# A weight-gradient matmul: one slice instead of two over the hardware queues, three more warm-up matmuls, and another order of the parts from slice 12 on

## The chip, the cores and the metric

The kernel runs on one core of a Trainium2 chip. The time is the device time of one execution in microseconds. Ten executions of the kernel before took 176.77 to 177.47 us; their median is 176.97 us.

## The reference

The input has the shape 16 x 512 x 1024 and the output's gradient 16 x 512 x 768, both float32. The result is the gradient of the weights, 1024 x 768, float32:

```python
grad_weight = np.einsum('bmk,bmn->kn', input, grad_output)
```

Batch and rows together make 8192 rows, which are summed over. So this is one product, the transposed input (1024 x 8192) times the gradient (8192 x 768).

## The kernel before, in words

The 8192 rows are cut into S = 64 slices of 128 rows. A slice has an X part (128 x 1024, from the input) and a G part (128 x 768, from the gradient). TensorE multiplies in bfloat16 and sums in float32 in PSUM, which has eight banks of 128 x 512 float32. Each slice takes twelve matmuls of 128 x 128 by 128 x 512. They belong to three parts of four groups each, and each group needs a bank of its own:

- part A, the output rows 0 to 511 and the columns 0 to 511: the weights of the matmul are four 128-column pieces of X, the moving side is G's first 512 columns (`wide_mm`, L129 to L132);
- part B, the same for the output rows 512 to 1023;
- part N, the output columns 512 to 767, turned: the weights are two 128-column pieces of G, the moving side is each half of X (`narrow_mm`, L134 to L143).

Three parts need twelve banks, and there are eight. So a part is opened, takes in some slices, and is closed: its four sums are evacuated from PSUM, and its banks go to the end of the list `free`. The first evacuation of a part is a copy, shared between VectorE and ScalarE (`copy_out`, L123); each later one is an addition on VectorE into `acc` or `acct` in SBUF (`add_out`, L120).

The order of the work is written out by hand. The scheduler is set to keep the program's order on TensorE, VectorE and ScalarE (L67). `ORDER` (L16) is a list of steps: "B15" means that part B takes in slices up to number 15 (not included), "AB16" that A and B take turns slice by slice, and "!" that the parts are closed after the last slice. After slice 12 the parts are opened and closed in turn up to slices 19, 31 and 50, and N takes the slices 31 to 63 in one run at the end of `ORDER`. A loop then finishes A and B (L210 to L222): for each of the eight groups it runs the slices 50 to 63 into one bank, adds the bank to `acc` and stores the result through the SyncE queue. The last group is cut into pieces of 256, 128 and 128 columns. N's result is turned by VectorE (L183) and stored through ScalarE's queue (L204).

The slices reach SBUF in two ways. Slices 0 and 1 come as float32 over the two hardware queues: SyncE issues G (L73, L75, L77), ScalarE issues X (L74, L76, L78). Each is then rounded to bfloat16 by VectorE and ScalarE in pieces of 256 columns (`round_pair`, L102; `round_slice`, L106). Slice 1's last 256 G columns (`gn1`, L89) and all of the slices 2 to 63 come over GpSimd's software queue, which rounds on the way in (L94 for G, L95 for X). The tiles `gt` and `xt` have 42 buffers each. At most eight transfers of this queue are in flight: each waits for the landing of the one eight places before it.

Before its first data has landed, TensorE runs nine 128 x 512 matmuls on constants into a bank that nobody reads (L84, L85).

Of the kernel before, what the change touches and what calls it, by code (L numbers as in the profile page):

```python
# [8 lines left out]
P = 128  # L9
NA = 512  # L10
SQ = 32

ORDER = (  # L16
    "A1! N1 B2! N2 A2 N3! A3 B3 A4! B5 N5 B6! N7 A6 N8! A9! B10 N9 B12! N12! A12! "
    "B15 A15 AB16 A19! B19! N19! A22 B22 AB28 A31! B31! N31! A34 B34 AB47 A50! B50! N64!"
).split()

HW = 2
WARMUP = 9
XBUFS = 42


# [1 line left out]
def kernel(  # L27
# [6 lines left out]
    nc = tc.nc  # L34
    bf16 = mybir.dt.bfloat16
    f32 = mybir.dt.float32

    B, M, K = input.shape
    _, _, N = grad_output.shape
    S = B * M // P  # L40
    KS = K // P
    NB = N - NA
# [3 lines left out]
    X = input.rearrange("b m k -> (b m) k")  # L46
    G = grad_output.rearrange("b m n -> (b m) n")
    OUT = out.rearrange("(ks p) n -> p ks n", p=P)

    head = ctx.enter_context(tc.tile_pool(name="head", bufs=1))  # L50
    xg = ctx.enter_context(tc.tile_pool(name="xg", bufs=XBUFS))
    accp = ctx.enter_context(tc.tile_pool(name="accp", bufs=1))
    psum = ctx.enter_context(tc.tile_pool(name="psum", bufs=1, space=bass.MemoryType.PSUM))
# [5 lines left out]
    turned = accp.tile([P, K // SQ, SQ, NT], f32, name="turned")  # L59


    xs = [None] * S
    gwide = [None] * S
    gnarrow = [None] * S
# [1 line left out]
    E = mybir.EngineType  # L66
    ctx.enter_context(tc.manual_schedule(engines={E.PE, E.DVE, E.Activation}))  # L67

    xf = [head.tile([P, K], f32, name=f"xf{s}") for s in range(HW)]
    gf = [head.tile([P, NA], f32, name=f"gf{s}") for s in range(HW)]  # L70
    gnf = head.tile([P, NB], f32, name="gnf")
    rows = [slice(s * P, (s + 1) * P) for s in range(HW)]
    nc.sync.dma_start(out=gf[0], in_=G[rows[0], 0:NA])  # L73
    nc.scalar.dma_start(out=xf[0][:, 0:NA], in_=X[rows[0], 0:NA])  # L74
    nc.sync.dma_start(out=gnf, in_=G[rows[0], NA:N])  # L75
    nc.scalar.dma_start(out=xf[0][:, NA:K], in_=X[rows[0], NA:K])  # L76
    nc.sync.dma_start(out=gf[1], in_=G[rows[1], 0:NA])  # L77
    nc.scalar.dma_start(out=xf[1], in_=X[rows[1], :])  # L78


    ones = nc.const_aps.tensor(1.0, (P, P), bf16)
    ones_wide = nc.const_aps.tensor(1.0, (P, NA), bf16)
    wps = psum.tile([P, NA], f32, name="bank7")
    for i in range(WARMUP):  # L84
        nc.tensor.matmul(wps, ones, ones_wide, start=(i == 0), stop=(i == WARMUP - 1))  # L85


    gn1 = head.tile([P, NB], bf16, name="gn1")
    nc.gpsimd.dma_start(out=gn1, in_=G[rows[1], NA:N])  # L89
    gnarrow[1] = gn1  # L90
    for s in range(HW, S):
        gt = xg.tile([P, N], bf16, name="gt")
        xt = xg.tile([P, K], bf16, name="xt")
        nc.gpsimd.dma_start(out=gt, in_=G[s * P : (s + 1) * P, :])  # L94
        nc.gpsimd.dma_start(out=xt, in_=X[s * P : (s + 1) * P, :])  # L95
        xs[s] = xt
        gwide[s] = gt[:, 0:NA]
        gnarrow[s] = gt[:, NA:N]

    QX = 256  # L100

    def round_pair(dst, src, c):  # L102
        nc.vector.tensor_copy(out=dst[:, c : c + QX], in_=src[:, c : c + QX])  # L103
        nc.scalar.copy(out=dst[:, c + QX : c + 2 * QX], in_=src[:, c + QX : c + 2 * QX])  # L104

    def round_slice(s):  # L106
        gt = head.tile([P, NA], bf16, name=f"g{s}")
        xt = head.tile([P, K], bf16, name=f"x{s}")
        round_pair(gt, gf[s], 0)

        for c in (0, NA) if s == 0 else (NA, 0):
            round_pair(xt, xf[s], c)
            if s == 0 and c == 0:
                gn0 = head.tile([P, NB], bf16, name="gn0")
                nc.vector.tensor_copy(out=gn0, in_=gnf)
                gnarrow[0] = gn0
        xs[s] = xt
        gwide[s] = gt

    def add_out(dst, src):  # L120
        nc.vector.tensor_add(out=dst, in0=src, in1=dst)  # L121

    def copy_out(dst, src, i):  # L123
        if i % 2 == 0:
            nc.vector.tensor_copy(out=dst, in_=src)  # L125
        else:
            nc.scalar.copy(out=dst, in_=src)  # L127

    def wide_mm(bank, k, s, start, stop, c0=0, c1=NA):  # L129
        nc.tensor.matmul(  # L130
            bank, xs[s][:, k * P : (k + 1) * P], gwide[s][:, c0:c1], start=start, stop=stop
        )  # L132
# [12 lines left out]
    class Part:  # L145
        def __init__(self, matmul, groups, dst):
            self.matmul = matmul
            self.groups = groups
            self.dst = dst
            self.done = 0  # L150
            self.first = True
            self.banks = None

    wide_dst = lambda k: acc[:, k, :]
    narrow_dst = lambda t, h: acct[:, t, h * NA : (h + 1) * NA]
    parts = {
        "A": Part(wide_mm, [(k,) for k in range(KS // 2)], wide_dst),
        "B": Part(wide_mm, [(k,) for k in range(KS // 2, KS)], wide_dst),
        "N": Part(narrow_mm, [(t, h) for h in range(KH) for t in range(NT)], narrow_dst),
    }  # L160
    free = [f"bank{i}" for i in range(8)]

    def one_slice(part, close):
        s = part.done
        part.done += 1
        if s < HW and xs[s] is None:
            round_slice(s)
        opened = part.banks is None
        if opened:
            names = [free.pop(0) for _ in part.groups]  # L170
            part.banks = [(name, psum.tile([P, NA], f32, name=name)) for name in names]
        for i, (group, (name, bank)) in enumerate(zip(part.groups, part.banks)):
            part.matmul(bank, *group, s, opened, close)
            if close:
                dst = part.dst(*group)
                if part.first:
                    copy_out(dst, bank, i)
                else:
                    add_out(dst, bank)
                if part is parts["N"] and s == S - 1:  # L180
                    t, h = group
                    hb = NA // SQ
                    nc.vector.transpose(  # L183
                        out=turned[:, h * hb : (h + 1) * hb, :, t],
                        in_=dst.rearrange("p (b r) -> p b r", r=SQ),
                    )
                free.append(name)
        if close:
            part.banks = None
            part.first = False  # L190

    for step in ORDER:
        close = step.endswith("!")
        names = step.rstrip("!").rstrip("0123456789")
        upto = int(step.strip("ABN!"))
        while any(parts[n].done < upto for n in names):
            for n in names:
                if parts[n].done < upto:
                    one_slice(parts[n], close and parts[n].done == upto - 1)

    rows_of = out.rearrange("(b r) n -> r b n", r=SQ)
    for a in range(P // SQ):
        c = NA + a * NT * SQ
        nc.scalar.dma_start(  # L204
            out=rows_of[:, :, c : c + NT * SQ],
            in_=turned[a * SQ : (a + 1) * SQ].rearrange("p b r t -> p b (r t)"),
# [3 lines left out]
    for k in range(KS):  # L210
        slices = range(parts["A" if k < KS // 2 else "B"].done, S)
        pieces = [(0, NA)] if k < KS - 1 else [(0, 256), (256, 384), (384, NA)]
        for c0, c1 in pieces:
            name = free.pop(0)
            bank = psum.tile([P, NA], f32, name=name)[:, 0 : c1 - c0]
            for s in slices:
                wide_mm(bank, k, s, s == slices[0], s == slices[-1], c0, c1)
            add_out(acc[:, k, c0:c1], bank)
            free.append(name)
            W = NB if k < 4 else c1 - c0  # L220
            for c in range(c0, c1, W):
                nc.sync.dma_start(out=OUT[:, k, c : c + W], in_=acc[:, k, c : c + W])  # L222

# [29 lines left out]
```

## Time and profile before

| | us |
|---|---|
| median of ten runs | 176.97 |
| lowest, highest | 176.77, 177.47 |
| the profiled execution, its own time | 176.86 |
| its span, first to last instruction | 175.1 |
| TensorE busy (matmuls) | 170.4 |
| VectorE busy | 53.9 |
| ScalarE busy | 6.7 |
| GpSimd busy (issuing transfers) | 66.6 |

The profile is of one execution. All times in its views are microseconds from the start of the span, and 1.76 us of the execution's own time lie outside the span. PE stands for TensorE's matmuls, PEld for its weight loads, which overlap the matmuls; DVE is VectorE, ACT ScalarE, POOL GpSimd and SP SyncE. A q behind an engine's name means its queue, and an L number is a line of the kernel. Matmuls are pipelined: the record of one is 379 ns long, though the next starts 216 ns later, so a matmul's pace is read from the distance between starts, and a wait from a distance that is too long.

The granted clock in the page is 1.00 for the whole span. The transfers keep the DMA engines busy from the first microseconds to about 145 us, and the stores of the result follow from 153 us on.

### The profile page before, as it was taken

How to read it: one execution, taken by the hardware profiler on the slowest of the kernel's cores; microseconds unless marked ns; L12 is line 12 of the kernel's file. 1: busy time of each engine (PE TensorE's matmuls, PEld its weight loads, DVE VectorE, ACT ScalarE, POOL GpSimd, SP SyncE). 2: the span in 40 equal slices, each digit the busy share in tenths (PEclk: the TensorE clock that was granted, in tenths of full speed). 3: DMA queues.
4: the chain of work that ended last, by engine and by line, in shares of the span. 5: the costliest groups of instructions: out<-in, count | busy, mean ns of one | idle time of the engine just before them, and what ended most of it. 6: DMA issues, size and time to landing. Idle time of an engine off the chain costs nothing.

```text
span 175.1 us, 1984 instructions
## 1 busy us (share of the span) xinstructions
PE 170.4 (97%) x790; PEld 78.0 (45%) x805; DVE 53.9 (31%) x91; ACT 6.7 (4%) x13; POOL 66.6 (38%) x129
## 2 busy tenths in 40 slices
PE   8999999999999999999999999999999999999993
PEld 2344444444444444444444444444444444444463
DVE  0565574790374100280320000047000003932122
ACT  3560000000000000000000000000000000000000
POOL 7444443444444444444444444444274200000000
DMA  5999999999999999999999999999999990077513
GB/s 168 318 208 207 209 208 208 208 208 208 208 208 209 208 208 209 208 207 210 207 208 208 208 209 209 208 208 209 208 208 208 208 188 7 0 185 193 165 60 120
DMA packets 25048, 33.48 MB, mean 191 GB/s; under 512 B 6480, under 2 KB 16080, under 8 KB 25040
## 3 DMA queue, kind: packets, MB, share of 16 engines
q0 software_dynamic: 18000, 28.52, 89.1%
q10 hardware_dynamic: 4592, 2.10, 4.6%
q1 hardware_dynamic: 2448, 2.75, 4.6%
q8 instruction: 6, 0.10, 0.2%
q14 instruction: 2, 0.02, 0.0%
HBM read 58.72 MB, written 3.15 MB: 353 GB/s over the span
## 4 chain that ended last, share of the span: by engine, by line
PE 93%; DMA 4%; issue 1%; SPq 0%; DVE 0%
PE bank L130 62%; PE bank L137 31%; DMA gf<-in_grad_output_dram 4%; SPq L75 0%; SPq L73 0%; DVE g L103 0%; DVE acc L121 0%; DVE x L103 0%
## 5 line engine op out<-in xcount | busy, mean ns | idle before, releaser
L130 PE MATMUL bank<-gt,xt 128*128 128x512 bf16 (+2 forms) x513 | 108.1, 367 | 0.6
L130 PEld LDWEIGHTS <-xt 128*128 128x128 bf16 x524 | 50.1, 98 | 57.4 <-DMA xt<-in_input_dram 0.7
L121 DVE TENSOR_TENSOR acc<-bank,acc 128x512 f32<-128x512 f32 (+2 forms) x54 | 33.1, 665 | 71.7 <-PE bank L130 71.2
L137 PE MATMUL bank<-xt,gt 128*128 128x512 bf16 x244 | 54.8, 379 | 0.2
L95 POOL DMA_DIRECT2D xt<-in_input_dram x62 | 33.0, 532 | 35.6 <-DMA xt<-in_input_dram 35.1
L94 POOL DMA_DIRECT2D gt<-in_grad_output_dram x62 | 33.0, 533 | 34.2 <-DMA gt<-in_grad_output_dram 30.9
L137 PEld LDWEIGHTS <-gt 128*128 128x128 bf16 x248 | 24.2, 98 | 29.3
L121 DVE TENSOR_TENSOR acct<-bank,acct 128x512 f32<-128x512 f32 x20 | 12.6, 679 | 39.4 <-PE bank L137 39.3
L130 PE MATMUL bank<-g,x 128*128 128x512 bf16 x16 | 5.0, 442 | 0.3 <-DVE x L103 0.3
L85 PE MATMUL bank<-const-bfloat16-1.0 128*128 128x512 bf16 x9 | 4.0, 629 | 0.8 <-PEq L237 0.8
L130 PEld LDWEIGHTS <-x 128*128 128x128 bf16 x16 | 1.5, 106 | 3.4 <-DVE x L103 1.7
L183 DVE STREAM_TRANSPOSE turned<-acct 128x512 f32<-128x512 f32 x4 | 2.9, 714 | 0.1
L125 DVE COPY acc<-bank 128x512 f32<-128x512 f32 x4 | 2.6, 680 | 0.3 <-PE bank L130 0.3
L85 PEld LDWEIGHTS <-const-bfloat16-1.0 128*128 128x128 bf16 x9 | 1.2, 142 | 2.7 <-issue 2.7
L103 DVE CAST g<-gf 128x256 bf16<-128x256 f32 x2 | 0.6, 296 | 5.4 <-DMA gf<-in_grad_output_dram 5.4
L127 ACT COPY acc<-bank 128x512 f32<-128x512 f32 x4 | 2.2, 587 | 0.4 <-PE bank L130 0.4
L137 PE MATMUL bank<-x,gn 128*128 128x512 bf16 x8 | 2.2, 399 | 0.0
L125 DVE COPY acct<-bank 128x512 f32<-128x512 f32 x2 | 1.3, 686 | 1.3 <-PE bank L137 1.3
L104 ACT CAST x<-xf 128x256 bf16<-128x256 f32 x4 | 1.5, 400 | 0.6 <-DMA xf<-in_input_dram 0.6
L137 PEld LDWEIGHTS <-gn 128*128 128x128 bf16 x8 | 0.9, 111 | 1.4 <-issue 0.5
L104 ACT ACT_TABLE_LOAD x1 | 1.3, 1283 | 2.2 <-issue 2.2
L103 DVE CAST x<-xf 128x256 bf16<-128x256 f32 x4 | 1.1, 298 | 0.1
(8 smaller groups left out, 3.2 us busy)
## 6 DMA issues: line engine op xcount, KB each, us to landing
xt<-in_input_dram POOLq DMA_DIRECT2D x62, 256.0 KB, 8.5
gt<-in_grad_output_dram POOLq DMA_DIRECT2D x62, 192.0 KB, 8.5
out_dram<-acc SPq DMA_DIRECT2D x9, 128.0 KB, 2.9
out_dram<-turned ACTq DMA_DIRECT2D x4, 256.0 KB, 3.2
out_dram<-acc SPq DMA_DIRECT2D x3, 256.0 KB, 2.0
gf<-in_grad_output_dram SPq DMA_DIRECT2D x2, 256.0 KB, 5.0
xf<-in_input_dram ACTq DMA_DIRECT2D x2, 256.0 KB, 3.9
xf<-in_input_dram ACTq DMA_DIRECT2D x1, 512.0 KB, 6.7
```

Source lines behind the costliest of these rows:

```text
L85: nc.tensor.matmul(wps, ones, ones_wide, start=(i == 0), stop=(i == WARMUP - 1))
L94: nc.gpsimd.dma_start(out=gt, in_=G[s * P : (s + 1) * P, :])
L95: nc.gpsimd.dma_start(out=xt, in_=X[s * P : (s + 1) * P, :])
L103: nc.vector.tensor_copy(out=dst[:, c : c + QX], in_=src[:, c : c + QX])
L104: nc.scalar.copy(out=dst[:, c + QX : c + 2 * QX], in_=src[:, c + QX : c + 2 * QX])
L121: nc.vector.tensor_add(out=dst, in0=src, in1=dst)
L125: nc.vector.tensor_copy(out=dst, in_=src)
L127: nc.scalar.copy(out=dst, in_=src)
L130: nc.tensor.matmul(bank, xs[s][:, k * P : (k + 1) * P], gwide[s][:, c0:c1], start=start, stop=stop)
L137: nc.tensor.matmul(bank, gnarrow[s].rearrange("p (r t) -> p t r", t=NT)[:, t], xs[s][:, h * NA : (h + 1) * NA], start=start, stop=stop,)
L183: nc.vector.transpose(out=turned[:, h * hb : (h + 1) * hb, :, t], in_=dst.rearrange("p (b r) -> p b r", r=SQ),)
```

## The change

It has five pieces.

1. Only slice 0 comes over the hardware queues, with two transfers on each. Slice 1 comes over GpSimd's queue, rounded on the way in, as the later slices do. It takes the first two places in that queue, and `gn1` is gone.
2. The roundings of slice 0 are written ahead of all the steps. Their order on VectorE and ScalarE is the one of before.
3. Three matmuls with 128 columns follow the nine of the warm-up. Each of the twelve is a sum of its own (`start` and `stop` are set on all).
4. `ORDER` is another from slice 12 on. A and B are closed at 17, 26, 41 and 50, and N at 17, 26 and 41. A step in small letters ("n17!") lets part N run bank by bank: all slices of the phase into the first bank, which is then evacuated while the second is filled, and so on (`bank_by_bank`). The sets before ended at 19, 31 and 50. VectorE gets twelve additions of 128 x 512 more.
5. The stores of the output groups 4 and 5 go out in halves of 256 columns, as those of 0 to 3 did already.

The diff, cut to its core:

```diff
 ORDER = (
     "A1! N1 B2! N2 A2 N3! A3 B3 A4! B5 N5 B6! N7 A6 N8! A9! B10 N9 B12! N12! A12! "
-    "B15 A15 AB16 A19! B19! N19! A22 B22 AB28 A31! B31! N31! A34 B34 AB47 A50! B50! N64!"
+    "B15 AB17! n17! AB26! n26! AB41! n41! AB47 A50! B50! N64!"
 ).split()
-HW = 2
-WARMUP = 9
+WARMUP = [512] * 9 + [128] * 3
...
-    nc.sync.dma_start(out=gf[0], in_=G[rows[0], 0:NA])
-    nc.scalar.dma_start(out=xf[0][:, 0:NA], in_=X[rows[0], 0:NA])
-    nc.sync.dma_start(out=gnf, in_=G[rows[0], NA:N])
-    nc.scalar.dma_start(out=xf[0][:, NA:K], in_=X[rows[0], NA:K])
-    nc.sync.dma_start(out=gf[1], in_=G[rows[1], 0:NA])
-    nc.scalar.dma_start(out=xf[1], in_=X[rows[1], :])
+    nc.sync.dma_start(out=gf[:, 0:NA], in_=G[0:P, 0:NA])
+    nc.scalar.dma_start(out=xf[:, 0:NA], in_=X[0:P, 0:NA])
+    nc.sync.dma_start(out=gf[:, NA:N], in_=G[0:P, NA:N])
+    nc.scalar.dma_start(out=xf[:, NA:K], in_=X[0:P, NA:K])
...
-    for i in range(WARMUP):
-        nc.tensor.matmul(wps, ones, ones_wide, start=(i == 0), stop=(i == WARMUP - 1))
+    for i, cols in enumerate(WARMUP):
+        nc.tensor.matmul(
+            wps[:, 0:cols],
+            ones,
+            nc.const_aps.tensor(1.0, (P, cols), bf16),
+            start=True,
+            stop=True,
+        )
...
-    nc.gpsimd.dma_start(out=gn1, in_=G[rows[1], NA:N])
-    gnarrow[1] = gn1
-    for s in range(HW, S):
+    for s in range(1, S):
...
+    round_pair(g0, gf, 0)
+    round_pair(xs[0], xf, 0)
+    nc.vector.tensor_copy(out=g0[:, NA:N], in_=gf[:, NA:N])
+    round_pair(xs[0], xf, NA)
...
+    def bank_by_bank(part, upto):
+        first = part.done
+        part.done = upto
+        for i in range(len(part.groups)):
+            open_bank(part, i)
+            for s in range(first, upto):
+                add_slice(part, i, s, s == first, s == upto - 1)
...
-            W = NB if k < 4 else c1 - c0
+            W = NB if k < 6 else c1 - c0
```

`add_slice` and `open_bank` are the body of `one_slice` (L163) for one group, and `slice_by_slice` runs the other steps as the loop at L192 did.

More of the change, by code (lines that the diff above doesn't have):

```diff
@@ L67 @@
     ctx.enter_context(tc.manual_schedule(engines={E.PE, E.DVE, E.Activation}))
[L69 to L73, printed above, removed]
-    nc.scalar.dma_start(out=xf[0][:, 0:NA], in_=X[rows[0], 0:NA])
-    nc.sync.dma_start(out=gnf, in_=G[rows[0], NA:N])
-    nc.scalar.dma_start(out=xf[0][:, NA:K], in_=X[rows[0], NA:K])
-    nc.sync.dma_start(out=gf[1], in_=G[rows[1], 0:NA])
-    nc.scalar.dma_start(out=xf[1], in_=X[rows[1], :])
+    xf = head.tile([P, K], f32, name="xf")
+    gf = head.tile([P, N], f32, name="gf")
+    nc.sync.dma_start(out=gf[:, 0:NA], in_=G[0:P, 0:NA])
+    nc.scalar.dma_start(out=xf[:, 0:NA], in_=X[0:P, 0:NA])
+    nc.sync.dma_start(out=gf[:, NA:N], in_=G[0:P, NA:N])
+    nc.scalar.dma_start(out=xf[:, NA:K], in_=X[0:P, NA:K])
     ones = nc.const_aps.tensor(1.0, (P, P), bf16)
-    ones_wide = nc.const_aps.tensor(1.0, (P, NA), bf16)
     wps = psum.tile([P, NA], f32, name="bank7")
-    for i in range(WARMUP):
-        nc.tensor.matmul(wps, ones, ones_wide, start=(i == 0), stop=(i == WARMUP - 1))
-    gn1 = head.tile([P, NB], bf16, name="gn1")
-    nc.gpsimd.dma_start(out=gn1, in_=G[rows[1], NA:N])
-    gnarrow[1] = gn1
-    for s in range(HW, S):
+    for i, cols in enumerate(WARMUP):
[7 more added lines that the diff above has]
+    for s in range(1, S):
         gt = xg.tile([P, N], bf16, name="gt")
@@ L98 @@
         gnarrow[s] = gt[:, NA:N]
+    xs[0] = head.tile([P, K], bf16, name="x0")
+    g0 = head.tile([P, N], bf16, name="g0")
+    gwide[0] = g0[:, 0:NA]
+    gnarrow[0] = g0[:, NA:N]
     QX = 256
@@ L104, in round_pair @@
         nc.scalar.copy(out=dst[:, c + QX : c + 2 * QX], in_=src[:, c + QX : c + 2 * QX])
[L106 to L118, printed above, removed]
+    round_pair(g0, gf, 0)
+    round_pair(xs[0], xf, 0)
+    nc.vector.tensor_copy(out=g0[:, NA:N], in_=gf[:, NA:N])
+    round_pair(xs[0], xf, NA)
     def add_out(dst, src):
@@ L151, in __init__ @@
             self.first = True
-            self.banks = None
+            self.banks = {}
     wide_dst = lambda k: acc[:, k, :]
@@ L161, with open_bank @@
     free = [f"bank{i}" for i in range(8)]
[L163 to L189, printed above, removed]
-            part.first = False
+    def open_bank(part, i):
+        name = free.pop(0)
+        part.banks[i] = (name, psum.tile([P, NA], f32, name=name))
@@ new lines, in add_slice @@
+    def add_slice(part, i, s, first, last):
+        group = part.groups[i]
+        name, bank = part.banks[i]
+        part.matmul(bank, *group, s, first, last)
+        if not last:
+            return
+        dst = part.dst(*group)
+        if part.first:
+            copy_out(dst, bank, i)
+        else:
+            add_out(dst, bank)
+        if part is parts["N"] and s == S - 1:
+            t, h = group
+            hb = NA // SQ
+            nc.vector.transpose(
+                out=turned[:, h * hb : (h + 1) * hb, :, t],
+                in_=dst.rearrange("p (b r) -> p b r", r=SQ),
+            )
+        free.append(name)
+        del part.banks[i]
+        if not part.banks:
+            part.first = False
@@ new lines, in slice_by_slice @@
+    def slice_by_slice(names, upto, close):
+        while any(parts[n].done < upto for n in names):
+            for n in names:
+                part = parts[n]
+                s = part.done
+                if s == upto:
+                    continue
+                part.done += 1
+                first = not part.banks
+                for i in range(len(part.groups)):
+                    if first:
+                        open_bank(part, i)
+                for i in range(len(part.groups)):
+                    add_slice(part, i, s, first, close and s == upto - 1)
@@ L192 @@
+    def bank_by_bank(part, upto):
+        first = part.done
+        part.done = upto
+        for i in range(len(part.groups)):
+            open_bank(part, i)
+            for s in range(first, upto):
+                add_slice(part, i, s, s == first, s == upto - 1)
     for step in ORDER:
@@ L194 @@
         names = step.rstrip("!").rstrip("0123456789")
[L195 to L199, printed above, removed]
+        upto = int(step.rstrip("!").lstrip("ABNn"))
+        if names.islower():
+            bank_by_bank(parts[names.upper()], upto)
+        else:
+            slice_by_slice(names, upto, close)
     rows_of = out.rearrange("(b r) n -> r b n", r=SQ)
```

## The prediction

> **What bounds the kernel now.** I read the page's head and its chain first: they say which engine the end hangs on.
>
> ```profile
> span 175.1 us, 1984 instructions
> PE 170.4 (97%) x790; PEld 78.0 (45%) x805; DVE 53.9 (31%) x91; ACT 6.7 (4%) x13; POOL 66.6 (38%) x129
> PE 93%; DMA 4%; issue 1%; SPq 0%; DVE 0%
> PE bank L130 62%; PE bank L137 31%; DMA gf<-in_grad_output_dram 4%; SPq L75 0%; SPq L73 0%; DVE g L103 0%; DVE acc L121 0%; DVE x L103 0%
> ```
>
> TensorE is the bound; DVE at 31% is not. A kernel that is 93% matmuls can gain only in TensorE's pauses, so I look for those. The chain in order of time (start, length, what) shows where it leaves TensorE:
>
> ```profile
> 1.64 6.57 DMA gf<-in_grad_output_dram
> 8.23 0.30 DVE g L103
> 8.53 0.21 DVE x L103
> 8.74 0.05 issue
> 8.79 1.04 PE bank L130 x4
> ```
>
> So everything up to 8.79 us hangs on one transfer, slice 1's `gf` (L77), which lands only at 8.2 us, and on its rounding. From 8.79 to 172.3 us the chain is matmuls. The timeline of the weight loads shows the start matmul by matmul:
>
> ```profile
> 3.71 0.15 PEld L85 LDWEIGHTS <-const-bfloat16-1.0 128*128 128x128 bf16 x1 [0.27 <-issue]
> 4.72 0.13 PEld L130 LDWEIGHTS <-x 128*128 128x128 bf16 x2 [0.86 <-DVE x L103]
> 6.41 0.15 PEld L137 LDWEIGHTS <-gn 128*128 128x128 bf16 x1 [0.28 <-issue]
> 6.78 0.31 PEld L137 LDWEIGHTS <-gn 128*128 128x128 bf16 x2 [0.22 <-issue]
> 7.21 0.75 PEld L130 LDWEIGHTS <-x 128*128 128x128 bf16 x4
> 8.78 0.55 PEld L130 LDWEIGHTS <-x 128*128 128x128 bf16 x4 [0.82 <-DVE x L103]
> ```
>
> The starts are 0.427 us apart up to 6.41 and 0.216 from 6.78: the clock doubles at about 6.73 (solved from the 0.373 step between them). The last warm-up matmul starts at 4.14 and streams to 4.57, the first real one starts at 4.73: pause 0.16. Slice 0 is done at 8.08 + 0.216 = 8.29, slice 1 starts at 8.785: pause 0.49.
>
> The waits of TensorE's loads name the only other pause:
>
> ```profile
> PEld L130 <- DMA xt<-in_input_dram: 0.7, 2, 0.4
> ```
>
> Of these two, the one at 46.0 us costs 0.085 us of matmul time (loads 0.502 and 0.015 apart where two steps are 0.432), the one at 72.7 nothing. I set the landing of each slice (trace) against the matmul that first needs it: slice 18 has no slack, slice 30 has 0.06 us, slice 11 has 0.66 (lands 30.53, B needs it at 31.24), the others over 1.2.
>
> **What the skill says.** "TensorE: Matmul & The Clock Gate", Part 1: the array runs at half clock until it has been busy through one window of about 3.4 us, and the window runs free of the kernel. The trace agrees on the two paces (0.427, 0.216); release came 5.95 us after the first warm-up matmul, so about one and three quarter windows. "DMA: Bandwidth & Descriptors", Queues, rings and completion order: every DMA engine takes turns between the queues with work, packet by packet. The trace agrees: slice 2's G (GpSimd's queue) started at 5.89 us beside slice 1's hardware transfers and took until 8.28; alone, such a one takes about 1 us.
>
> **The change, part by part.**
>
> *Warm-up.* Three 128-column matmuls follow the nine. At half clock that is a quarter of 0.427 each, 0.107 (the clock page's back-to-back price is the same), so 0.32 us: the array is busy to 4.57 + 0.32 = 4.89, while slice 0's data is ready at 4.73. So it starts 0.16 later; below nothing is possible only if the closed gap brings the clock release forward, above, 0.3 if small loads don't overlap. I take 0.16. With release still at 6.73: (6.73 - 4.89)/0.427 = 4.3 matmuls at the slow pace, the other 7.7 of slice 0's twelve at 0.216: slice 0 ends at 6.73 + 1.66 = 8.39, 0.1 later than now.
>
> *Slice 1 over GpSimd's queue.* The 768 KB hardware pair (L77, L78), `gn1` and six casts go. The first software packet moved at 4.64 us (the queue view has none up to 4.6), the second transfer's at 5.89. Slice 1's G takes the place of the first: 0.97 us alone plus 0.25 beside slice 0's last hardware packets (to 5.0), so to 5.86; X starts at 5.89, and as slice 2's X took 1.99 us from first packet to landing (7.85 to 9.84), lands at 7.9. Bounds: 7.6 if the queue is ready sooner, 9.84 if the second transfer can't land before the one in that place does now. B's slice 1 then starts at the later of 8.39 and 7.95: 8.39, against 8.785. Gain 0.39 us. X and G arrive rounded, so no DVE or ACT step stands between; what is late next is slice 0 itself.
>
> *The stream behind it.* Slice 2's X follows 2.2 us (POOL's rows for X: 14.54, 16.70, 18.95, 21.11) after slice 1's: 10.1 against 9.84, all later slices 0.2 later (range -0.1 to +0.5), since this queue never rests. TensorE is 0.39 earlier. Slice 11's slack: 0.66 - 0.39 - 0.2 = 0.07, just held. Slices 2 to 10: over 0.6.
>
> *Order from slice 12 on.* The matmul count is the same. A and B alone eat a slice in 8 x 0.216 = 1.73 us, faster than 2.2, so slack falls by 0.5 a slice and jumps when N fills in. Replaying the new order against the landings: 0.86 at slice 16, then 6.4 falling to 2.4 (17 to 25), 9.6 to 3.0 (26 to 40), over 9 to slice 49; the end is as before. Minus 0.6, still positive: the 0.085 pause at 46 us goes, no new one comes.
>
> *Twelve more evacuations* x 0.66 = 7.9 us of DVE, 31% to 36%, beside matmuls. Uncovered they would cost where a bank is late. Tightest: `n17` ends, its last bank is wanted by B's fourth group 8 x 0.216 = 1.73 us after that matmul starts; it ends 0.38 after, the add takes 0.69: 0.6 to spare. `n26` takes A's first bank with 0.66 to spare. Cost 0. Bank-by-bank runs keep 0.216: the closing loop runs so already.
>
> *Edits at nothing.* SP and ACT lose one issue each (0.42, 0.45); ACT's table load moves up, but its first cast waits for `gf` at 4.1. Banks 4 and 5 are written in halves: two more SP issues of 0.33, behind adds 3 us apart and done before the last add at 172.32; if SP were backed up, 0.3 to 0.7.
>
> **Sum.** 0.39 + 0.085 = 0.48 off the end of the matmuls. The profiled execution: span 175.10 + 1.76 around it = 176.86; less 0.48, 176.4. The median of the ten runs is 0.11 above it, 176.97: forecast 176.5.
>
> **Rivals.**
> 1. *The clock decides.* Now the pause before 8.785 swallows any release up to about 7.7 us; afterwards nothing does. If the window falls so that release is at 7.6 (start plus two windows), slice 0 ends at 8.82 and only the 0.085 and noise are left: 176.9. If early (under 6.6), slice 11's landing sets the end: with the stream 0.1 early it is 171.2 for 172.04, 176.1. For it: the page's free window; against: I see one release only.
> 2. *The stream eats it.* Landings 0.4 to 0.7 later: slice 11 ends at 30.53 + 0.5 + 0.05 = 31.1, gain 0.15: 176.8. For it: the 1.4 us wait of POOL at 27.47, a hiccup that slack 0.07 won't take.
> 3. *The other side: the software queue starts slowly.* If slice 1's X can't land before the transfer in second place does now, 9.84, B starts at 9.9, 1.1 later, the stream is 2.2 late and slice 11 slips by 2.2 - 0.66 = 1.5; less the 0.085 that is 1.4 over now: 178.4. It decides from the point where the stream is 0.74 late (0.66 + 0.085), which is a landing of slice 1's X at 8.4. For it: the queue moved nothing from 5.4 to 5.85 us, after its first transfer's packets; against: the ones that follow shared with 768 KB of hardware traffic that is gone.
> 4. *It doesn't do what it says*: the new order and loads stand in the build's instruction list, so only the gap is in doubt; that the warm-up ends after the data is counted above.
>
> **How the numbers follow.** A difference under 0.2% (0.35 us) can't be told from none. Forecast (gain 0.36 to 0.65) 0.50; early release with a quick stream (176.1 to 176.3) 0.12; rivals 1 late and 2 (176.62 to 177.3) 0.27; rival 3 0.11. Faster 0.62, same 0.27, slower 0.11. The range 176.1 to 177.0 leaves out rival 3 and the tails.
>
> **What would show it.** Right: chain without a gf piece of 6 us; B's slice 1 at 8.2 to 8.5; no TensorE wait at 46 us; slice 1's X landing under 8.2; DVE with about 101 instructions. Wrong: TensorE loads waiting for `xt` before 12 us or near 31 us, a clock step after 7.2, waits for DVE after `n17` or `n26`, or a last store later than 1.9 us after the last add.

## The result, and the profile after

| | before | after |
|---|---|---|
| median, us | 176.94 (32 runs) | 176.15 (9 runs) |
| lowest to highest, us | 176.66 to 179.29 | 175.97 to 176.22 |
| profiled execution, own time and span, us | 176.86, 175.1 | 176.08, 174.3 |

The ratio of after to before is 0.9948, with a 95% interval of 0.993 to 0.9966: the kernel became faster by 0.5%, where 176.5 us, 0.27% under the median, was forecast. The direction was right and the time lies inside the range. The gain was 1.7 to 2 times the forecast: 0.79 us by the medians, 0.5% by the ratio, where 0.47 us was forecast. One of the runs of before took 179.29 us; without it the ratio of the means is 0.9952, so it decides nothing here.

The head of the page and its chain, after:

```profile
span 174.3 us, 2009 instructions
PE 169.2 (97%) x793; PEld 77.9 (45%) x808; DVE 61.2 (35%) x100; ACT 5.5 (3%) x10; POOL 67.1 (39%) x130
PE 93%; DMA 3%; issue 1%; POOL 0%; DVE 0%; POOLq 0%
PE bank L124 62%; PE bank L131 31%; DMA xt<-in_input_dram 3%; POOL gt L93 0%; DVE acc L115 0%; POOLq L252 0%
```

TensorE is still the bound. VectorE went from 53.9 to 61.2 us busy (twelve further additions, three roundings fewer) and appears in the chain only with the last addition. The chain in order of time (start, length, what) has another first link:

```profile
1.90 6.06 DMA xt<-in_input_dram
7.95 0.05 issue
8.00 1.04 PE bank L124 x4
```

Slice 1's X comes from GpSimd's queue, lands at 7.95 us, and B's slice 1 starts at 8.00 instead of 8.79. No rounding stands between the two any more. The timeline of the weight loads over the same stretch:

```profile
3.29 0.15 PEld L81 LDWEIGHTS <-const-bfloat16-1.0 128*128 128x128 bf16 x1 [0.28 <-issue]
3.61 0.60 PEld L81 LDWEIGHTS <-const-bfloat16-1.0 128*128 128x128 bf16 x4 [0.17 <-issue]
4.72 0.55 PEld L124 LDWEIGHTS <-x 128*128 128x128 bf16 x4 [0.51 <-DVE x L106]
5.39 0.74 PEld L131 LDWEIGHTS <-g 128*128 128x128 bf16 x4
6.97 0.10 PEld L124 LDWEIGHTS <-x 128*128 128x128 bf16 x1 [0.19 <-issue]
8.00 0.55 PEld L124 LDWEIGHTS <-xt 128*128 128x128 bf16 x4 [0.93 <-DMA xt<-in_input_dram]
```

Here is the surprise. Four loads in 0.55 us at 4.72 is the fast pace: the clock was released inside the warm-up, at about 3.50 us (solved from the 0.320 us between the matmuls of 3.29 and 3.61: a matmul takes 0.427 us before the release and 0.216 after it), against 6.73 in the profile of before. So the last warm-up matmuls were short, slice 0 started at 4.73 as before, and it was done at 7.40 instead of 8.29. It then waited 0.6 us for slice 1's X.

The waits of the weight loads for data in the whole execution (us, times, longest):

```profile
PEld L124 <- DMA xt<-in_input_dram: 1.6, 3, 0.9
```

And the one of them that cost time later on, in the timeline:

```profile
30.55 0.55 PEld L124 LDWEIGHTS <-xt 128*128 128x128 bf16 x4 [0.43 <-DMA xt<-in_input_dram]
```

The three waits are slice 1's (0.9), slice 11's at 30.55 us (0.43 in the load, 0.108 us of matmul time) and one at 41.66 that costs nothing. The wait at 46 us is gone. The account of the end: 0.786 us from the start, plus 0.085 from 46 us, less 0.108 at 30.55, makes 0.763; the last matmul starts at 171.304 us instead of 172.065, 0.761 earlier.

### The profile page after: what moved, and what is told of

It is laid out like the page before. It is cut to its first block, busy times and chain, and to the rows that moved or that the text cites. A ratio compares the mean times of both kernels' runs of the same rounds, so it can differ in the third digit from the quotient of the medians.

```text
span 174.3 us, 2009 instructions
## 1 busy us (share of the span) xinstructions
PE 169.2 (97%) x793; PEld 77.9 (45%) x808; DVE 61.2 (35%) x100; ACT 5.5 (3%) x10; POOL 67.1 (39%) x130
## 4 chain that ended last, share of the span: by engine, by line
PE 93%; DMA 3%; issue 1%; POOL 0%; DVE 0%; POOLq 0%
PE bank L124 62%; PE bank L131 31%; DMA xt<-in_input_dram 3%; POOL gt L93 0%; DVE acc L115 0%; POOLq L252 0%
## 5 line engine op out<-in xcount | busy, mean ns | idle before, releaser
L124 PE MATMUL bank<-gt,xt 128*128 128x512 bf16 (+2 forms) x523 | 110.5, 368 | 0.9 <-DMA xt<-in_input_dram 0.4
L115 DVE TENSOR_TENSOR acc<-bank,acc 128x512 f32<-128x512 f32 (+2 forms) x62 | 37.9, 667 | 73.5 <-PE bank L124 73.0
L131 PE MATMUL bank<-xt,gt 128*128 128x512 bf16 x246 | 55.9, 379 | 0.3
L93 POOL DMA_DIRECT2D gt<-in_grad_output_dram x63 | 33.7, 535 | 27.8 <-DMA gt<-in_grad_output_dram 24.9
L115 DVE TENSOR_TENSOR acct<-bank,acct 128x512 f32<-128x512 f32 x24 | 15.7, 682 | 30.0 <-PE bank L131 29.9
L81 PE MATMUL bank<-const-bfloat16-1.0 128*128 128x512 bf16 (+1 forms) x12 | 3.6, 472 | 0.8 <-PEq L252 0.8
L124 PE MATMUL bank<-g,x 128*128 128x512 bf16 x8 | 2.1, 380 | 0.3 <-ACT x L107 0.3
L124 PEld LDWEIGHTS <-x 128*128 128x128 bf16 x8 | 0.7, 98 | 1.3 <-DVE x L106 0.5
L121 ACT COPY acct<-bank 128x512 f32<-128x512 f32 x2 | 1.1, 588 | 1.5 <-PE bank L131 1.5
L131 PE MATMUL bank<-x,g 128*128 128x512 bf16 x4 | 1.0, 379 | 0.0
```

The costliest lines, as they stand in the source:

```text
L81: nc.tensor.matmul(wps[:, 0:cols], ones, nc.const_aps.tensor(1.0, (P, cols), bf16), start=True, stop=True,)
L124: nc.tensor.matmul(bank, xs[s][:, k * P : (k + 1) * P], gwide[s][:, c0:c1], start=start, stop=stop)
L131: nc.tensor.matmul(bank, gnarrow[s].rearrange("p (r t) -> p t r", t=NT)[:, t], xs[s][:, h * NA : (h + 1) * NA], start=start, stop=stop,)
```

## The experiments

Theory 1: the gain is the earlier start of slice 1, and it survives only because the new order no longer needs slice 18 at 46 us; when the clock is released is chance. Its rivals: the pieces add up by themselves, the order alone brings the gain, or the new warm-up brings the release forward.

**Slice 1 alone.** The changed kernel with these two edits (and `start` and `stop` of the warm-up as before):

```diff
-    "B15 AB17! n17! AB26! n26! AB41! n41! AB47 A50! B50! N64!"
+    "B15 A15 AB16 A19! B19! N19! A22 B22 AB28 A31! B31! N31! A34 B34 AB47 A50! B50! N64!"
-WARMUP = [512] * 9 + [128] * 3
+WARMUP = [512] * 9
```

> The changed kernel with the order and the nine warm-up matmuls of before: slice 1 over GpSimd's queue alone (stores in halves kept). Theory 1 (each piece needs the other): B's slice 1 starts at about 8.0 to 8.4 us instead of 8.8, but the old order wants slice 18 at 46 us, which lands at 45.95 as before, so TensorE waits there for all that it had gained, 0.4 to 0.8 us, and the matmuls end at 172.0 to 172.1: 176.9 us, no change. Theory 2 (the pieces add up): the early start is kept to the end, 176.2 to 176.5 us, with no wait at 46 us over 0.1 us.

176.91 us against 177.02, ratio 0.9997 (0.9988 to 1.0005): nothing. The timeline of its weight loads near 46 us:

```profile
44.96 0.10 PEld L124 LDWEIGHTS <-xt 128*128 128x128 bf16 x1
46.17 1.41 PEld L124 LDWEIGHTS <-xt 128*128 128x128 bf16 x8 [1.11 <-DMA xt<-in_input_dram]
```

In the profile of before, the same load waited less:

```profile
45.99 0.98 PEld L130 LDWEIGHTS <-xt 128*128 128x128 bf16 x6 [0.40 <-DMA xt<-in_input_dram]
```

B's slice 1 had started at 7.93, 0.85 us early. TensorE then waited 0.33 us at 30.69 for slice 11 and 0.79 us at 46.17 for slice 18. All that was won at the start was given back there, and in this execution 0.18 us more (the last matmul started at 172.24). Slice 18's X lands at 45.86 to 46.13 us in all the thirteen profiles, however early slice 1 starts. Theory 1 holds: slice 18's landing sets the end of the old order.

**The order alone.** The kernel before with the new line of `ORDER` and `bank_by_bank`.

> The kernel before with the new order from slice 12 on and bank-by-bank runs, nothing else. Theory 1: only the 0.085 us wait at 46 us goes; B's slice 1 still starts at about 8.8 us, matmuls end at 171.95, 176.85 us. Theory 2 (the new order itself brings the gain, through fewer waits for banks or transfers): 176.1 to 176.5 us with the start unchanged.

176.78 us, ratio 0.9992 (0.9983 to 1.0). The chain starts as before:

```profile
1.65 6.73 DMA gf<-in_grad_output_dram
8.96 1.04 PE bank L130 x4
```

B's slice 1 started at 8.96, after slice 1's `gf`, and no wait followed. In the trace the order alone takes away the 0.085 us at 46 us and nothing else; the times, whose interval reaches to 0.3 us, don't contradict it.

**The warm-up alone.** The kernel before with the twelve warm-up matmuls of the change.

> The kernel before with the new warm-up (three more small matmuls, start and stop set on all), nothing else. Both theories: 176.9 us, since slice 1's gf lands at 8.2 us whatever the clock does. They differ in when the step of the weight loads goes from 0.427 to 0.216 us. Theory 1 (the window falls by chance): anywhere from 3.3 to 7.6 us in any kernel. Theory 2 (the new warm-up brings the release forward by a window): 3.3 to 4.2 us here and in every kernel that has it, 6.5 to 7.6 in every kernel with the old one.

177.1 us, ratio 1.0005 (0.9996 to 1.0014). The weight loads:

```profile
4.57 0.25 PEld L85 LDWEIGHTS <-const-bfloat16-1.0 128*128 128x128 bf16 x2 [0.28 <-issue]
4.78 0.71 PEld L136 LDWEIGHTS <-x 128*128 128x128 bf16 x4
5.62 0.74 PEld L143 LDWEIGHTS <-gn 128*128 128x128 bf16 x4
```

The release came at 5.04 us, later than the 4.2 that theory 2 gave as its limit for this warm-up. Slice 0 was then done at 7.56 and TensorE waited 1.2 us for slice 1: an earlier clock is worth nothing while `gf` sets the start. Slice 0's first matmul started at 4.89 us, the 0.16 late that the prediction had worked out for a half-clock warm-up.

**The change without its warm-up.**

```diff
-WARMUP = [512] * 9 + [128] * 3
+WARMUP = [512] * 9
```

(with `start` and `stop` as before)

> The changed kernel with the nine warm-up matmuls of before, all else new. Theory 1 (release by chance, and slice 11's landing at 30.5 us sets the end whenever release comes before about 6.5 us): 176.1 to 176.2 us like the changed kernel, or up to 0.3 us more in runs where release is late; TensorE waits 0.1 us near 30.5 us if release was early. Theory 2 (the new warm-up brings release forward): release at 6.5 to 7.6 us, B's slice 1 at 8.3 to 8.8 us, no wait at 30.5 us, 176.4 to 176.9 us in most runs.

176.2 us, ratio 0.9951 (0.9938 to 0.9963), the same as the whole change. Three of the weight loads:

```profile
4.72 0.55 PEld L124 LDWEIGHTS <-x 128*128 128x128 bf16 x4 [0.85 <-DVE x L106]
7.69 0.55 PEld L124 LDWEIGHTS <-xt 128*128 128x128 bf16 x4 [0.63 <-DMA xt<-in_input_dram]
30.44 0.55 PEld L124 LDWEIGHTS <-xt 128*128 128x128 bf16 x4 [0.62 <-DMA xt<-in_input_dram]
```

The release came before 4.72 us with the old warm-up too, B's slice 1 started at 7.70, and slice 11 was waited for at 30.44, 0.30 us. So slice 1 and the order together make the gain, and the warm-up has no part in it that could be measured.

**A late release, forced.**

```diff
-WARMUP = [512] * 9 + [128] * 3
+WARMUP = [512] * 2
```

> The changed kernel with a warm-up of two 512-column matmuls instead of twelve, so that TensorE stands idle from about 1.6 to 4.7 us and the clock release must come late. Theory 1 (the start now follows the clock): with a release at T, slice 0 ends at 7.32 + 0.494 x (T - 4.73), and what that is past 8.0 us is on the end, less the 0.1 us wait that goes at 30.5 us: T between 7.5 and 11 us, B's slice 1 at 8.7 to 10.4 us, 176.7 to 178.4 us. Rival (the slack ahead of slice 11 swallows the clock, as the pause of before did): 176.1 to 176.4 us whatever T is.

177.34 us over 22 runs, from 176.61 to 178.24; ratio 1.0019 (1.0006 to 1.0033). The weight loads of the profiled execution:

```profile
7.27 0.15 PEld L131 LDWEIGHTS <-g 128*128 128x128 bf16 x1 [0.28 <-issue]
7.70 0.15 PEld L124 LDWEIGHTS <-x 128*128 128x128 bf16 x1 [0.28 <-issue]
8.13 0.61 PEld L124 LDWEIGHTS <-x 128*128 128x128 bf16 x3 [0.28 <-issue]
```

The release came at 8.29 us. The formula (twelve matmuls at 0.216 us from 4.73, and 0.494 us more for each us at the slow pace) gives 7.32 + 0.494 x 3.56 = 9.08 for B's slice 1; it started at 9.07, so nothing but the clock held it up. The last matmul started at 172.25, 0.95 us after the changed kernel's: 1.07 from the start, less the 0.11 at slice 11 that was no longer waited for. The runs spread over 1.63 us, where the changed kernel has 0.25. By the formula that would be a release that moves by 3.3 us from one execution to the next; one execution was profiled, so this is not shown. So a warm-up of two matmuls is too short here, and rival 1 of the prediction was a real risk. Nine leave little of it: releases over the profiles with nine or twelve lay at 3.5 to 6.7 us, and slice 11's landing hides all but the two latest (the 0.1 us there is used up by a release at 6.3, by the formula). Numbers between two and nine were not tried.

**More slack for slices 11 and 16, first attempt.** In `ORDER`:

```diff
-B10 N9 B12! N12! A12! B15 AB17! n17!
+B10 N9 B11 N11 B12! N12! A12! B13 AB17! n17!
```

> The changed kernel with two small changes of order: N takes slices 9 and 10 before B takes slice 11 (B11 N11 B12 instead of B12), and A and B alternate from slice 13 instead of 15, so that slices 11 and 16 are wanted 1.7 us later. Theory 1 (the landing of slice 11 holds the end): the 0.1 us wait at 30.5 us goes, none comes, matmuls end at 171.2, 176.05 us where the changed kernel has 176.15; more where slice 1 lands early (at 7.7: 0.3 us). Rival (the wait there only takes the place of another further on): 176.15 us, with a wait for xt or a bank elsewhere.

178.16 us, ratio 1.0067 (1.0055 to 1.0079). The expectation failed. The wait at 30.5 us did go, but new ones came at 34.64, 38.23 to 39.42 and 53.15 us, 2.1 us in all. The waits of the stretch from 38 to 40 us:

```profile
PEld L124 <- issue: 1.3, 3, 0.5
...
PE bank L124 <- DVE acc L115: 0.4, 2, 0.2
```

I had replayed the order against the landings only. With N closing four matmuls after B, and A soon after, parts are reopened before VectorE has emptied their banks, at 0.65 us each.

**The same, with slice 1's X in two transfers.**

```diff
-        nc.gpsimd.dma_start(out=xt, in_=X[s * P : (s + 1) * P, :])
+        for c in (NA, 0) if s == 1 else (0,):
+            w = NA if s == 1 else K
+            nc.gpsimd.dma_start(out=xt[:, c : c + w], in_=X[s * P : (s + 1) * P, c : c + w])
```

> The kernel of the run before with slice 1's X sent in two transfers of 512 columns, B's half first. Theory 1: that half lands at about 7.1 us, so B's slice 1 follows slice 0 at 7.4 if the clock was released early; of the 0.55 us gained 0.2 to 0.3 is given back where slices 2, 4 and 6 land (slack 0.4, 0.3 and 0.2 us): matmuls end at 170.9 to 171.0, 175.8 us. Rival (two transfers of narrower rows delay the stream, so that the slices behind land later by as much): 176.0 to 176.2 us.

178.09 us, ratio 1.0062 (1.0051 to 1.0074), with the same waits for banks, and not the 175.8 to 176.2 us of either theory. The waits cover the question; it was asked again below.

**N slice by slice.** The changed kernel with "N17!", "N26!" and "N41!" for "n17!", "n26!" and "n41!".

> The changed kernel with N slice by slice (as before the change) in place of bank by bank at 17, 26 and 41. If running bank by bank is what keeps TensorE from waiting for evacuations: N's third and fourth bank are wanted at 0.43 us intervals after A and B have closed together, while VectorE frees one each 0.65 us, so 0.5 to 0.7 us is lost after 26 and again after 41, little after 17: 177.2 to 177.5 us. If it makes no difference (the banks are free anyway): 176.15 us.

178.94 us, ratio 1.0111 (1.0097 to 1.0124), 2.8 us over the changed kernel. TensorE pauses by 0.58 us five times, at 50.95, 66.2, 75.41, 101.03 and 115.41 us. The timeline from 64 us on shows one of them:

```profile
64.26 4.88 DVE L115 TENSOR_TENSOR acc<-bank,acc 128x512 f32<-128x512 f32 x8 [12.77 <-PE bank L124]
...
66.20 0.10 PEld L131 LDWEIGHTS <-gt 128*128 128x128 bf16 x1 [0.32 <-issue]
66.80 2.54 PE L131 MATMUL bank<-xt,gt 128*128 128x512 bf16 x10 [0.22 <-DVE acc L115]
```

Eight additions in a row take VectorE 4.88 us, and N, which wants its banks 0.216 us apart, waits for them. I expected two such waits, and 177.2 to 177.5 us, and found five: the reopening of B after N (50.95, 75.41, 115.41) waits in the same way. The new phases pay only with N bank by bank.

**More slack, second attempt.** An order that was replayed against the banks as well:

```diff
-B10 N9 B12! N12! A12! B15 AB17! n17!
+B10 N10 B12! N12! A12! B15 AB16! n16!
```

> The changed kernel with N up to 10 instead of 9 before B takes slices 10 and 11, and the first phase closed at 16 instead of 17. This gives slices 11 and 16 more slack and was replayed against the banks too (VectorE frees one each 0.65 us; the tightest bank has 0.1 us to spare). Theory 1 (slice 11's landing holds the end): the wait at 30.5 us is gone and no other comes, matmuls end at 170.9 to 171.2 depending on slice 1's landing (7.7 to 8.0), 175.8 to 176.0 us. Rival (the slack only moves the wait): 176.15 us, with waits for xt or banks between 34 and 50 us.

175.85 us, ratio 0.9937 (0.9924 to 0.9949); lowest 175.74, highest 176.19. The weight loads around slice 11 run through in the timeline:

```profile
30.00 1.61 PEld L124 LDWEIGHTS <-xt 128*128 128x128 bf16 x8
31.73 1.61 PEld L131 LDWEIGHTS <-gt 128*128 128x128 bf16 x8
```

The waits of the whole execution hold one for data, slice 1's:

```profile
PEld L124 <- DMA xt<-in_input_dram: 0.6, 1, 0.6
```

The last matmul starts at 170.95, 0.35 us before the changed kernel's. Here slice 1's X landed at 7.71, and the 0.24 us of it were kept to the end, which the changed kernel would have lost at slice 11, as the run without its warm-up did. In that run B's slice 1 started 0.30 us earlier than in the changed kernel, and the last matmul only 0.11 us earlier (171.19). So slice 11's landing is what held the changed kernel's end. The medians, 175.85 and 176.15, differ by 0.3 us; the two intervals against before overlap at their ends, so the times alone do not settle it, while the trace does.

**That order, with slice 1's X in two transfers.**

> The run before with slice 1's X in two transfers, B's half first. Theory 1: with an early release B's slice 1 follows slice 0 at 7.4 us, and 0.1 to 0.4 us of it is given back at the landings of slices 2, 4 and 6: matmuls end at 170.9 us, 175.75 us, 0 to 0.25 us under the run before. Rival (the narrower rows delay the stream): equal to the run before or up to 0.2 us over it.

175.97 us, ratio 0.9949 (0.9936 to 0.9963): the rival held. The first half landed at 7.46 and not at 7.1, only 0.25 us before the whole X of the run before, and slice 2's X at 10.36 instead of 9.93. TensorE waited at 10.40, 14.81 and 19.22 us, 0.37 in all. In this execution the release (5.15 us) also left slice 0 running to 7.62, so the half could not have been used earlier.

**The stores of groups 4 and 5 whole.** `k < 4` again in place of `k < 6`.

> The changed kernel with output groups 4 and 5 stored whole, as before. Theory 1 (the halves cost and bring nothing, since these stores are done before the last group's addition): 176.15 us, the time from the last addition to the end of the span unchanged at 2.75 us. Rival (the two further issues or the narrower rows delay the last stores): 0.3 us less.

176.29 us, ratio 0.9956 (0.9943 to 0.9968), not to be told from the changed kernel. From the start of the last addition to the end of the span it took 2.87 us, against 2.75. One profile doesn't settle 0.1 us; the halves bring little or nothing.

## Why the prediction was right or wrong, point by point

- *TensorE's pauses are all there is to gain, and slice 1 is the large one.* Right: slice 1 gave 0.79 us at the start; with the 0.085 won at 46 us and the 0.108 lost at slice 11, 0.76 reached the end.
- *Slice 1's X lands at 7.9.* The number was right: 7.95 (7.65 to 8.21 over the eight profiles that sent it whole). Its parts were not, and that they cancel was luck: the first packet of X moved at 5.52 us instead of 5.89, beside the last ones of slice 1's G, and it took 2.43 us from there to the landing instead of 1.99.
- *"B's slice 1 then starts at the later of 8.39 and 7.95: 8.39."* This step failed. The 8.39 took the release at 6.73 us from one profile for a fixed time. In the changed kernel it came at 3.50, slice 0 was done at 7.40 instead of 8.39, and the landing at 7.95 decided: B's slice 1 started at 8.00, a gain of 0.79 us instead of 0.39. The section of the Trainium skill quoted there ("TensorE: Matmul & The Clock Gate", Part 1) says that the window runs free; the runs here agree that the release moves. The profiles here with nine or twelve warm-up matmuls show 3.50, 3.79, before 4.72, 4.47, 4.51, 5.04, 5.15, 5.63, 5.88, 6.16, 6.63 and 6.73 us. Of the seven of them that send slice 1's X whole over GpSimd's queue, five have slice 0 done before X lands. The quoted rule of one whole busy window of 3.4 us does not hold for the earliest two: they came 2.7 and 3.0 us after the first warm-up matmul. The early release was listed as a half of rival 1, at 0.12, because "I see one release only". Spread evenly over one window of 3.4 us, which that section gives, from one window after the start (4.2 us) to two (7.6), a release comes before the 6.6 us of that rival in seven cases of ten: an estimate from the figure of that section, and it would have put the rival first. Two of the signs that the prediction set for being wrong did appear: TensorE loads waited for `xt` before 12 us and near 31 us.
- *The warm-up costs 0.16 us.* Right where the clock is still slow at its end (4.89 us in the warm-up alone), nothing where it isn't (4.73 in the changed kernel). It brought nothing that these runs could measure either.
- *The stream is 0.2 us late behind slice 1.* It was 0.30 late at slice 2 (10.14 for 9.84) and 0.29 at slice 8, but level at slice 11 (30.51 for 30.53). So "all later slices 0.2 later" failed from slice 10 on. The slack was the 0.66 of before; the start took 0.79, and 0.108 was waited. In all the thirteen profiles slice 11's X lands at 30.40 to 30.66 us, while slice 2's lands anywhere from 9.84 to 10.43: a late start of the stream was not passed on to slice 11. Slices 2 to 10 had 0.27 us or more to spare, where over 0.6 was forecast. Between slices 8 and 10 both kernels show a hiccup, after which the 16 parts of a transfer land 1.3 us apart, and there the difference goes; why, the traces don't tell, and no run tried it.
- *Order from slice 12 on.* Right: the 0.085 at 46 us goes, no bank is waited for, and the closest landing after slice 12 is slice 16's (0.17 us before the matmul that needs it). What the text did not say is that the old order would have eaten the whole gain at slice 18; it counted the order at 0.085 us, and the run with slice 1 alone shows that it is worth the whole 0.8.
- *Twelve additions at nothing.* Right, and so is the reason given: after `n17` B's fourth group starts 0.62 us after its bank was emptied, where 0.6 was forecast. What happens without such time to spare, two runs show: 2.8 us lost with N slice by slice, 2.1 us with the first other order.
- *Rival 3, the software queue starts slowly.* It didn't: the second transfer's packets (from 5.52 us) did not wait for the end of the first one's (6.02).

## What to carry to other kernels

Before counting a pause as a gain, follow the earlier start through every later landing: a stage with no slack further on takes it all back, and two edits that measure nothing alone can be worth 0.8 us together. Replay a new order against both the landings and the emptying of banks, since the one that gave slack for data lost 2 us to banks. And a time seen once in one profile, such as a clock release, is a sample; write down its spread before resting a forecast on it.

## What the runs showed of the hardware that was not expected

The release of TensorE's clock moved by more than 3 us between executions of the same first nine matmuls (3.50 to 6.73 us). The profile's granted clock reads 1.00 (0.998 in two) in all of them, so only the distance between matmuls shows it. A transfer of half the columns by GpSimd's queue did not land in half the time: at 7.46 and 7.55 us in the two profiles with 512 columns, at 7.65 to 8.21 in the eight with 1024, from the same place in the queue. Where the half landed at 7.46, its last packet had ended at 6.72, 0.74 us before; a whole X that landed at 7.71 had its last at 7.39, 0.32 before.
